# A ring of 19 weight tiles in place of 15, and the expert gather set between weight tiles

## The chip, the core and the metric

The kernel runs on one core of one Trainium2 chip. The metric is the device time of one execution in microseconds (us), lower is better. All inputs lie in the chip's memory (HBM) in the layout that the host prepared; the kernel is one launch.

## The reference, cut to what matters

The model is a decoder trunk of two layers on 256 tokens of width 1024. Each layer has a mixer and then a channel mixer. Layer 0 has a dense SwiGLU; layer 1 has a mixture of eight experts, each token sent to two of them. The change touches only that last part:

```python
def moe_swiglu(x, w_router, w1, w3, w2):
    t = x.reshape(bn * s, d)
    logits = (t @ w_router).astype(jnp.float32)
    top_val, top_idx = lax.top_k(logits, TOP_K)
    top_w = jax.nn.softmax(top_val, axis=-1)
    combine = jnp.sum(jax.nn.one_hot(top_idx, N_EXPERTS) * top_w[..., None], axis=1)
    for e in range(N_EXPERTS):
        out = out + combine[:, e:e + 1] * swiglu(t, w1[e], w3[e], w2[e])
```

with `swiglu(x, w1, w3, w2) = (silu(x @ w1) * (x @ w3)) @ w2`. w1 and w3 of an expert are 1024 x 3584, w2 is 3584 x 1024, all in float32: 44 MB an expert, 352 MB of the 476 MB that the kernel moves.

## The kernel before, in words

The first 466 us are the two mixers and the dense channel mixer; at their end stand the second mixer's output product (lines 147 to 150, out of the split activations hy_hi and hy_lo), the router and the top-2 choice. What follows works through the experts one after the other.

**Weight tiles.** An expert's weights come as 46 tiles: 32 of 128 x 1792 floats (917,504 bytes; for each half of the 3584 columns eight of w1 and then eight of w3) and 14 of 128 x 2048 floats (1 MB) of w2. That makes 368 loads for eight experts. The class Weights (line 938) issues them from SP's queue, in order, at line 953. FIRST (line 34) names the buffers in the order in which they are first filled; "x" is used once, and after that the other 15 names go round as a ring. A load may leave when the tile that was in its buffer has been used, and when the eighth load before it has landed. Buffers A0 to A4 are the ones that the first 466 us also load into; a0 to a3 and b0 to b5 lie in memory that the mixers used before (the pools mg, mc, mw, ra, rb are opened one after the other in the place of the mixers' pools, and ra, which holds a0 to a3, comes behind mg, mc and mw).

**An expert.** Tokens of an expert sit in slots, at most CAP = 96, as G = 3 groups of 32, or as two groups if 64 slots are enough: a register (mask, read out of cnt) picks one of two versions of the expert's code, one with G = 3 and one with G = 2. With these inputs experts 1, 3 and 5 take three groups and the others two. The first HEAD = 3 tiles of an expert are always done with three groups. g1 (line 1090) multiplies the expert's slots xg with a w1 or w3 tile: 4 G matmuls of 448 columns, each on 32 of TensorE's columns; a profile counts two records for each. silu and gate (lines 1108 and 1114) make ga out of the sums, turn (line 1118) transposes ga into gT through a misc bank, and g2 (line 1144) multiplies gT with the w2 tiles. yfin and scatter bring the result back to the tokens; the scatter's four pieces stand after the first three tiles of the next expert.

**The gather.** For a pair of experts make_p (line 1016) builds Pm, a one-hot matrix from tokens to 2 x 128 slots. gather(p, d2) (line 1068) makes one quarter of the pair's slots: for two of the eight blocks of the width, four matmuls each (high part and low part of the scaled tokens, for two halves of the tokens) of 128 rows by 256 columns into one misc bank, then two copies to XG, one on ACT and one on DVE, that take 96 of each 128 slots. The first pair's four quarters stand together ahead of the first expert's first tile (line 1283); the other pairs' quarters stand after tiles 1 to 4 of the second g1 of experts 1, 3 and 5, that is after the expert's tiles 10 to 13. htk_h and htk_l are the scaled tokens split into a rounded high part (ACT) and a low part (DVE, line 1028), out of four PSUM banks tk; DVE makes them in four pieces of 512 columns, with make_p between the second and the third.

**PSUM.** Eight banks: six acc (c0 to c5) are allocated first and two misc (m0, m1) last, so the misc banks are the ones that were used by the last two of the tk tiles.

**On the chip's names.** PE is TensorE, DVE VectorE, ACT ScalarE, POOL GpSimd; SP issues the weight loads.

Of the kernel before, what the change touches and what calls it, by code (L numbers as in the profile page):

```python
# [8 lines left out]
F32 = mybir.dt.float32  # L9
F32R = mybir.dt.float32r  # L10
# [18 lines left out]
CAP = 96  # L29
G = CAP // 32  # L30
FH = 1792
HEAD = 3
FQ = 448
FIRST = ("x", "b1", "b2", "a0", "a1", "A0", "a2", "A1", "a3", "A2", "b0", "A3", "A4", "b3", "b4", "b5")
AHEAD = len(FIRST) - 2
ADAS2 = (0, 0, 0)
ADAS3 = (1, 1, 3)
# [14 lines left out]
def tile_trunk(ctx: ExitStack, tc: tile.TileContext, xT_d, c_d, vecs_d, ada0_d, ada_d, adar_d, adah_d, s1_d, s2_d,  # L52
# [797 lines left out]
    def ffn_body(fk):  # L850
# [59 lines left out]
        for d in range(KB):  # L910
# [3 lines left out]
            if d % 2:  # L914
# [16 lines left out]
    rk_p = bank("o")  # L931

    slots = {k: (ra if k[0] == "a" else rb).tile([P, 2048], F32, name="raw", tag=k)
             for k in ("a0", "a1", "a2", "a3", "b0", "b1", "b2", "b3", "b4", "b5")}
    slots.update({f"A{i}": raw_a() for i in range(RAW1)})
    slots["x"] = const.tile([P, 2048], F32, name="raw", tag="ex")

# [23 lines left out]
    wts = Weights()  # L961
    wts.upto(len(FIRST))

    ga = {(h, g): mg.tile([P, FQ], F32, name="ga", tag=f"ga{h}{g}") for h in range(2) for g in range(G)}
    gT = [mg.tile([P, 14, CAP], F32, name="gT", tag=f"gT{h}") for h in range(2)]
    PTm = mg.tile([P, 2, T], F32R, name="PTm")
    XG = [mw.tile([P, 2, KB, CAP], F32, name="xg", tag=f"xg{p}") for p in range(2)]
    scr = XG[1].rearrange("p e k s -> p (e k s)")
    Pm = mw.tile([P, 2, 2, P], F32R, name="Pm")
    Qw = mw.tile([P, 2, 2, P], F32, name="Qw")  # L970
    wsl = mw.tile([P, 2], F32, name="ws")
# [22 lines left out]
    for t in range(2):  # L994
# [14 lines left out]
    nc.vector.scalar_tensor_tensor(rk, rk_p[:, 0:16].rearrange("p (t e) -> p t e", t=2), 1.0, sel,  # L1009
                                   op0=OP.add, op1=OP.mult)  # L1010

    def make_p(p):
        return nc.vector.tensor_tensor(Pm, iotas[:, None, None, :].to_broadcast([P, 2, 2, P]),
                                       rk[:, :, 2 * p:2 * p + 2, None].to_broadcast([P, 2, 2, P]),
                                       op=OP.is_equal)

    tw = mc.tile([P, 2, 2], F32, name="tw")
    cmx = mc.tile([P, 8], F32, name="cmx")
    htk_h = mc.tile([P, 2, D], F32R, name="htk_h")
    htk_l = mc.tile([P, 2, D], F32R, name="htk_l")  # L1020
    for j in range(2):
        if j:
            p_ins = make_p(0)
        for t in range(2):
            hi = htk_h[:, t, 512 * j:512 * j + 512]
            nc.scalar.activation(hi, tk[j][t], AF.Copy, scale=rt[:, t:t + 1])
            with tc.issue_after((p_ins if j else sel_ins).ins):
                nc.vector.scalar_tensor_tensor(htk_l[:, t, 512 * j:512 * j + 512], tk[j][t], rt[:, t:t + 1],
                                               hi.bitcast(F32), op0=OP.mult, op1=OP.subtract)
# [12 lines left out]
    nc.vector.tensor_scalar(many[:, 7:8], many[:, 7:8], -1.0, 384.0, op0=OP.mult, op1=OP.add)  # L1042
    nc.vector.tensor_scalar(cmx[:, 2:3], cmx[:, 0:1], CAP + 0.5, many[:, 7:8], op0=OP.is_gt, op1=OP.mult)
    nc.vector.tensor_add(cmx[:, 1:2], cmx[:, 1:2], cmx[:, 2:3])
    nc.vector.tensor_copy(cnt, cmx)
    nc.vector.tensor_sub(tw, mx[:, :, 0:2], mx[:, :, 0:1].to_broadcast([P, 2, 2]))
    fin = nc.scalar.activation(tw, tw, AF.Exp)
    tables(fin, SILU)
# [8 lines left out]
    pps.close()  # L1057
    pm = moe.enter_context(tc.tile_pool(name="pm", bufs=1, space=PSUM, reuse_waits="tile"))

    acc = [pm.tile([P, 512], F32, name="acc", tag=f"c{i}") for i in range(6)]  # L1060
    ms_ = [pm.tile([P, 512], F32, name="misc", tag=f"m{i}") for i in range(2)]
    turn_ = [0]

    def misc():
        turn_[0] ^= 1
        return ms_[turn_[0]]

    def gather(p, d2):
# [9 lines left out]
        tv = tp.rearrange("p (d e s) -> p d e s", d=2, e=2)  # L1078
        for dd in range(2):
            d = 2 * d2 + dd  # L1080
            sh = mods(1, 3)[:, d:d + 1]
            if dd:
                r = nc.vector.tensor_scalar(XG[p % 2][:, :, d], tv[:, dd, :, 0:CAP], sh, None, op0=OP.add)
            else:
                nc.scalar.activation(XG[p % 2][:, :, d], tv[:, dd, :, 0:CAP], AF.Identity, bias=sh)
        return r

    ahead = []

# [24 lines left out]
    def gate(h, banks, G):
        for g in range(G):
            nc.vector.tensor_mul(ga[h, g], banks[g][:, 0:FQ], ga[h, g])  # L1116

    def turn(h, g):
        tp = misc()
        for b in range(4):  # L1120
            o = 128 * b if b < 3 else FQ - P
            nc.tensor.transpose(tp[:, b * P:(b + 1) * P], ga[h, g][:, o:o + P], ident)  # L1122
        sl = slice(32 * g, 32 * g + 32)
        nc.scalar.copy(gT[h][:, 0:12, sl].rearrange("p (c b) s -> p b c s", c=4),  # L1124
                       tp[:, 0:384].rearrange("p (b c s) -> p b c s", b=3, c=4))
        tl = tp[:, 384:512].rearrange("p (u v s) -> p u v s", u=2, v=2)
        for v in range(2):
            nc.vector.tensor_copy(gT[h][64 * v:64 * v + 64, 12:14, sl], tl[64:128, :, v])  # L1128
# [179 lines left out]

    for e in range(NE):
        lo, hi = (acc[0:3], acc[3:6]) if e % 2 == 0 else (acc[3:6], acc[0:3])  # L1310
        heavy = (mask >> e) & 1
# [5 lines left out]
        fill = {0: (0,), 1: (1, 2), 2: (3,)} if e else {}  # L1317
        g1(e, lo, {k: lambda cs=cs: [scatter(c) for c in cs] for k, cs in fill.items()}, G, 0, HEAD)
# [110 lines left out]
```

## Time and profile before

| what | us |
|---|---|
| median of three runs | 1343.88 |
| the three runs | 1343.88, 1343.93, 1340.54 |
| the profiled execution, own time | 1339.97 |
| its span in the trace | 1338.3 |
| PE busy in the span | 1261.2 (94%) |
| DVE busy | 488.5 (37%) |
| ACT busy | 308.4 (23%) |
| bytes moved by DMA | 476.01 MB, 356 GB/s over the span |

The span is the time from the first to the last instruction that the profiler saw; the execution's own time is 1.7 us more. A busy PE counts the time in which matmuls stream, also where one slow clock makes them last longer, so 94% is not 94% of what TensorE could do. The page cuts the span into 40 slices of 33.5 us each; slice 0 begins at 0 us and slice 14 at 468 us, about where the first expert begins.

### The profile page before, as it was taken

To read this page: it belongs to the slowest core of one execution; us is meant where nothing else is said; L and a number is where in the kernel's file an instruction comes from. 1 tells how busy PE (TensorE), PEld (TensorE's weight loads), DVE (VectorE), ACT (ScalarE), POOL (GpSimd) and SP (SyncE) were. 2 spreads that over 40 slices of the span, in tenths; PEclk is the share of its full clock that TensorE was granted. 3 is DMA by queue.
4 is the path that set the end of the run, shared out by engine and by line. 5 is a ranking of instruction groups with operands and counts; after the bars stand their busy time and mean duration, and the time that the engine had idled before them with its cause. 6 is when DMAs were issued, how large, how long until landed. Compare 5 with 4: busy or idle time off the path is not lost. (4 is left out here: it accounts for less than half of the span.)

```text
span 1338.3 us, 26935 instructions
## 1 busy us (share of the span) xinstructions
PE 1261.2 (94%) x11847; PEld 713.7 (53%) x11847; DVE 488.5 (37%) x940; ACT 308.4 (23%) x521; POOL 14.4 (1%) x42
## 2 busy tenths in 40 slices
PE   7999999999999999899999989999989999998985
PEld 6888799999888943243333334333324333333322
DVE  7899888886678421011101111101101111111012
ACT  5764544444476310001000001000000100000101
POOL 3000000000000000000000000000000000000000
PEclk9999999999989989999999989999999999998998
DMA  9868799887454959999998999998999999899993
GB/s 368 341 222 299 270 371 353 333 307 255 161 216 158 407 195 426 424 423 425 423 372 360 426 422 424 426 411 323 425 425 422 426 424 367 350 426 423 425 427 146
DMA packets 72208, 476.01 MB, mean 356 GB/s; under 512 B 8097, under 2 KB 9265, under 8 KB 44802
## 3 DMA queue, kind: packets, MB, share of 16 engines
q1 hardware_dynamic: 71568, 473.07, 88.0%
q8 instruction: 104, 1.70, 0.5%
q0 software_dynamic: 352, 0.84, 0.2%
q14 instruction: 38, 0.31, 0.1%
q10 hardware_dynamic: 146, 0.09, 0.0%
HBM read 472.92 MB, written 1.05 MB: 354 GB/s over the span
## 5 line engine op out<-in xcount | busy, mean ns | idle before, releaser
L1096 PE MATMUL acc<-raw,xg 128*32 128x448 f32 x4984 | 497.4, 552 | 19.0 <-issue 16.4
L1096 PEld LDWEIGHTS acc<-raw,xg 128*32 128x32 f32 x4984 | 164.7, 112 | 321.1 <-issue 304.4
L1154 PE MATMUL acc<-raw,gT 128*32 128x512 f32 x2128 | 238.7, 594 | 13.0 <-DMA raw<-in_moe_dram 12.8
L118 DVE TENSOR_TENSOR wlo<-raw,whi 128x1024 fp32r<-128x1024 f32 (+2 forms) x138 | 159.4, 1163 | 49.7 <-ACT whi L116 47.7
L116 ACT CAST whi<-raw 128x1024 fp32r<-128x1024 f32 (+2 forms) x138 | 137.3, 999 | 119.6 <-PE bk_b L148 74.2
L1154 PEld LDWEIGHTS acc<-raw,gT 128*32 128x32 f32 x2128 | 65.1, 110 | 170.5 <-issue 143.3
L147 PE MATMUL bk_b<-hy_hi,whi 128*128 128x256 f32 (+1 forms) x528 | 128.0, 282 | 3.9 <-DVE Am L610 2.6
L148 PE MATMUL bk_b<-hy_lo,whi 128*128 128x256 f32 (+1 forms) x528 | 126.1, 280 | 0.0
L223 DVE SCALAR_TENSOR_TENSOR junk<-raw,exA 128x1024 bf16<-128x1024 f32 x88 | 107.9, 1226 | 1.4 <-DMA raw<-in_ada_dram 0.5
L147 PEld LDWEIGHTS bk_b<-hy_hi,whi 128*128 128x128 f32 (+1 forms) x528 | 96.9, 185 | 5.7 <-DVE Am L610 2.8
L148 PEld LDWEIGHTS bk_b<-hy_lo,whi 128*128 128x128 f32 (+1 forms) x528 | 96.9, 185 | 0.5 <-DVE hy_lo L397 0.2
L1124 ACT COPY gT<-misc 128x384 f32<-128x384 f32 x38 | 18.2, 480 | 318.1 <-PE misc L1122 297.4
L1116 DVE TENSOR_TENSOR ga<-acc,ga 128x448 f32<-128x448 f32 x38 | 23.7, 625 | 168.9 <-PE acc L1096 166.2
L1110 ACT ACTIVATE ga<-acc 128x448 f32<-128x448 f32 x38 | 20.7, 544 | 241.7 <-PE acc L1096 241.4
L1169 DVE SCALAR_TENSOR_TENSOR yhl<-acc,ws,yhl 128x512 fp32r<-128x512 f32 x11 | 8.3, 751 | 185.3 <-ACT yhl L1168 185.3
L150 PE MATMUL bk_b<-hy_hi,wlo 128*128 128x256 f32 (+1 forms) x528 | 74.4, 280 | 0.0
L147 PE MATMUL bk_o<-hy_hi,whi 128*128 128x256 f32 x256 | 65.7, 285 | 4.8 <-ACT hy_hi L396 4.8
L148 PE MATMUL bk_o<-hy_lo,whi 128*128 128x256 f32 x256 | 65.6, 283 | 0.6 <-DVE hy_lo L397 0.3
L150 PEld LDWEIGHTS bk_b<-hy_hi,wlo 128*128 128x128 f32 (+1 forms) x528 | 66.0, 185 | 0.0
L1128 DVE COPY gT<-misc 64x64 f32<-64x64 f32 x76 | 17.2, 227 | 120.9 <-ACT gT L1124 119.9
L1185 DVE SCALAR_TENSOR_TENSOR xT<-misc,modc,xT 128x256 f32<-128x256 f32 x60 | 26.7, 481 | 80.4 <-PE misc L1180 80.3
L150 PE MATMUL bk_o<-hy_hi,wlo 128*128 128x256 f32 x256 | 54.8, 285 | 0.0
(272 smaller groups left out, 1065.8 us busy)
## 6 DMA issues: line engine op xcount, KB each, us to landing
raw<-in_moe_dram SPq DMA_DIRECT2D x256, 896.0 KB, 14.6
raw<-in_moe_dram SPq DMA_DIRECT2D x112, 1024.0 KB, 17.7
raw<-in_ada_dram SPq DMA_DIRECT2D x44, 1024.0 KB, 7.2
raw<-in_ffn_dram SPq DMA_DIRECT2D x33, 1024.0 KB, 6.7
raw<-in_s_dram SPq DMA_DIRECT2D x16, 776.0 KB, 6.4
raw<-in_s_dram SPq DMA_DIRECT2D x12, 1024.0 KB, 4.9
raw<-in_wo_dram SPq DMA_DIRECT2D x8, 1024.0 KB, 4.8
raw<-in_adah_dram SPq DMA_DIRECT2D x2, 1024.0 KB, 6.2
```

The costliest lines, as they stand in the source:

```text
L116: self.hi_ins = nc.scalar.copy(hi[:, :n], raw[:, c0:c1])
L118: self.lo_ins = nc.vector.tensor_sub(lo[:, :n], raw[:, c0:c1], hi[:, :n].bitcast(F32))
L147: nc.tensor.matmul(out, lhsT=wh, rhs=xh, start=start, stop=False, skip_group_check=True)
L148: nc.tensor.matmul(out, lhsT=wh, rhs=xl, start=False, stop=False, skip_group_check=True)
L150: nc.tensor.matmul(out, lhsT=wl, rhs=xh, start=False, stop=stop, skip_group_check=True)
L223: nc.vector.scalar_tensor_tensor(junk, row, 1.0, cond, op0=OP.mult, op1=OP.mult, accum_out=dots[:, l, 8 * g + k:8 * g + k + 1])
L1096: mm = nc.tensor.matmul(banks[g][32 * c:32 * c + 32, 0:FQ], lhsT=xg[:, k, 32 * g:32 * g + 32], rhs=raw[:, FQ * c:FQ * c + FQ], start=(k == ...
L1110: sil = nc.scalar.activation(ga[h, g], banks[g][:, 0:FQ], AF.Silu)
L1116: nc.vector.tensor_mul(ga[h, g], banks[g][:, 0:FQ], ga[h, g])
L1124: nc.scalar.copy(gT[h][:, 0:12, sl].rearrange("p (c b) s -> p b c s", c=4), tp[:, 0:384].rearrange("p (b c s) -> p b c s", b=3, c=4))
L1154: nc.tensor.matmul(yy[n][32 * c:32 * c + 32, :], lhsT=gt[:, blk, 32 * g:32 * g + 32], rhs=rhs, start=(j == 0 and (n == 1 or bb == 0)), sto ...
L1185: nc.vector.scalar_tensor_tensor(xT[:, d], tps[h][:, cols], mods(1, 5)[:, d:d + 1], xT[:, d], op0=OP.mult, op1=OP.add)
```

## The change

The diff below is cut to its core. What it does, part by part:

- FIRST gets 20 names: "x", used once, and 19 that go round. b6 to b9 are new, and the order of the names changes; a1 is the fifth name, a0 the last.
- ga has one set of three tiles instead of one for each half; XG is one tile with three slots, an expert's slot being e % 3, instead of two tiles with two; make_p makes two compares where the pair's slots come in the other order (pair).
- The second argument of the launch, dynamic_dma_scratch_size=2048, makes GpSimd's descriptor ring smaller.
- The eight PSUM banks are allocated in another order: m0 second, m1 sixth.
- A gather's matmul takes 2 x 96 columns of Pm instead of 2 x 128.
- The first pair's quarters are put between tiles: quarter 0 ahead of the first expert's first tile, quarters 1, 2 and 3 after its first, second and third tile. The load of mask follows the first tile, and weights() the third.
- The low parts are made in eight pieces of 256 columns (rest), with rk and make_p after the first of them and the counting between the fourth and the fifth.

```diff
-FIRST = ("x", "b1", "b2", "a0", "a1", "A0", "a2", "A1", "a3", "A2", "b0", "A3", "A4", "b3", "b4", "b5")
+FIRST = ("x", "b9", "b2", "b3", "a1", "a2", "A0", "a3", "A1", "b0", "A2", "b1", "A3", "A4", "b4", "b5", "b6", "b7", "b8",
+         "a0")
...
-             for k in ("a0", "a1", "a2", "a3", "b0", "b1", "b2", "b3", "b4", "b5")}
+             for k in [f"a{i}" for i in range(4)] + [f"b{i}" for i in range(10)]}
...
-    ga = {(h, g): mg.tile([P, FQ], F32, name="ga", tag=f"ga{h}{g}") for h in range(2) for g in range(G)}
+    ga = {g: mg.tile([P, FQ], F32, name="ga", tag=f"ga{g}") for g in range(G)}
...
-    XG = [mw.tile([P, 2, KB, CAP], F32, name="xg", tag=f"xg{p}") for p in range(2)]
-    scr = XG[1].rearrange("p e k s -> p (e k s)")
+    XG = mw.tile([P, 3, KB, CAP], F32, name="xg")
+    scr = XG[:, 2].rearrange("p k s -> p (k s)")
...
+    def rest(t, q, after):
+        cs, half = slice(T * q, T * q + T), slice(T * (q % 2), T * (q % 2) + T)
+        with tc.issue_after(after.ins):
+            return nc.vector.scalar_tensor_tensor(htk_l[:, t, cs], tk[q // 2][t][:, half], rt[:, t:t + 1],
+                                                  htk_h[:, t, cs].bitcast(F32), op0=OP.mult, op1=OP.subtract)
...
+    r_ins = rest(0, 0, sel_ins)
+    with tc.issue_after(r_ins.ins):
+        r_ins = nc.vector.scalar_tensor_tensor(rk, rk_p[:, 0:16].rearrange("p (t e) -> p t e", t=2), 1.0, sel,
+                                               op0=OP.add, op1=OP.mult)
...
+    def pair(p):
+        return sorted((2 * p, 2 * p + 1), key=lambda e: e % 3)
...
+    with tc.issue_after(r_ins.ins):
+        r_ins = make_p(0)
+    for t, q in ((1, 0), (0, 1), (1, 1)):
+        r_ins = rest(t, q, r_ins)
+    with tc.issue_after(r_ins.ins):
+        nc.vector.max(cmx, rk_p[:, 16:24])
...
-    nc.vector.tensor_copy(cnt, cmx)
+    c_ins = nc.vector.tensor_copy(cnt, cmx)
+    for t, q in ((0, 2), (1, 2), (0, 3), (1, 3)):
+        c_ins = rest(t, q, c_ins)
...
-    acc = [pm.tile([P, 512], F32, name="acc", tag=f"c{i}") for i in range(6)]
-    ms_ = [pm.tile([P, 512], F32, name="misc", tag=f"m{i}") for i in range(2)]
+    banks = [pm.tile([P, 512], F32, name="acc" if n[0] == "c" else "misc", tag=n)
+             for n in ("c0", "m0", "c1", "c2", "c3", "m1", "c4", "c5")]
+    acc, ms_ = [banks[i] for i in (0, 2, 3, 4, 6, 7)], [banks[i] for i in (1, 5)]
...
     def gather(p, d2):
-        tp = misc()
+        a, b = (e % 3 for e in pair(p))
+        tp = misc().rearrange("p (d t) -> p d t", d=2)[:, :, 0:2 * CAP]
...
-                    nc.tensor.matmul(tp[:, dd * T:(dd + 1) * T], lhsT=src[:, t, d * P:(d + 1) * P], rhs=Pm[:, t],
+                    nc.tensor.matmul(tp[:, dd], lhsT=src[:, t, d * P:(d + 1) * P], rhs=Pm[:, t, :, 0:CAP],
...
-    for d2 in range(4):
-        last = gather(0, d2)
-        if d2 == 0:
-            mask = nc.values_load(cnt[0:1, 1:2], min_val=0, max_val=256 + 127,
-    with tc.issue_after(last.ins):
-        weights()
...
+        if e == 0:
+            gather(0, 0)
+            g1(0, lo, {0: lambda: gather(0, 1)}, G, 0, 1)
+            mask = nc.values_load(cnt[0:1, 1:2], min_val=0, max_val=256 + 127,
...
+            fill = {k: lambda k=k: gather(0, k + 1) for k in (1, 2)}
+        g1(e, lo, fill, G, k0, HEAD)
         if e == 0:
+            weights()
...
-    nc = _bacc.Bacc("TRN2", target_bir_lowering=False, num_devices=1)
+    nc = _bacc.Bacc("TRN2", target_bir_lowering=False, num_devices=1, dynamic_dma_scratch_size=2048)
```

## Rows read from the trace of the kernel before

**Rows 1.** The profile's page: its span, and what DMA moved in 40 equal slices.
```profile
span 1338.3 us, 26935 instructions
...
GB/s 368 341 222 299 270 371 353 333 307 255 161 216 158 407 195 426 424 423 425 423 372 360 426 422 424 426 411 323 425 425 422 426 424 367 350 426 423 425 427 146
```

**Rows 2.** The chain that ended last: start us, us, what it was.
```profile
1241.69 18.00 DMA raw<-in_moe_dram
...
1296.45 19.46 DMA raw<-in_moe_dram
...
1316.05 1.98 PE acc L1154 x16
```

**Rows 3.** Busy times by stretch (us): length, engines' busy time, TensorE clock, DMA share, GB/s.
```profile
469.20:483.50 14.30, 11.89 (x86) 7.85 (x90) 6.47 (x22) 2.89 (x5) 0.00 (x0) 0.75 0.01 2
483.50:505.00 21.50, 21.50 (x232) 7.41 (x228) 0.40 (x1) 1.09 (x2) 0.00 (x0) 1.00 0.93 365
505.00:560.00 55.00, 52.46 (x502) 16.60 (x494) 5.96 (x16) 3.00 (x6) 0.00 (x0) 1.00 1.01 425
640.00:705.00 65.00, 63.76 (x608) 22.52 (x604) 9.64 (x22) 2.81 (x5) 0.00 (x0) 1.00 0.97 386
705.00:715.00 10.00, 10.00 (x112) 3.51 (x108) 0.55 (x2) 1.09 (x2) 0.00 (x0) 1.00 0.78 273
1080.00:1141.00 61.00, 59.77 (x556) 20.90 (x552) 8.99 (x21) 2.81 (x5) 0.00 (x0) 0.98 0.96 378
1141.00:1152.00 11.00, 11.00 (x116) 3.46 (x112) 0.00 (x0) 1.09 (x2) 0.00 (x0) 0.96 0.79 281
1152.00:1316.00 164.00, 148.05 (x1384) 48.43 (x1376) 16.96 (x41) 9.07 (x16) 0.00 (x0) 0.98 1.00 419
```

**Rows 4.** SP's queue, waits at 600 to 712, then 1215 to 1300: us, times, longest.
```profile
SPq L953 <- PE acc L1096: 61.8, 29, 6.5
...
SPq L953 <- DMA raw<-in_moe_dram: 53.7, 29, 2.6
```

**Rows 5.** PE's waits at 538 to 562, 764 to 779 and 982 to 997.
```profile
PE acc L1154 <- DMA raw<-in_moe_dram: 2.5, 5, 0.6
...
PE acc L1154 <- DMA raw<-in_moe_dram: 0.6, 1, 0.6
...
PE acc L1154 <- DMA raw<-in_moe_dram: 1.6, 3, 0.6
```

**Rows 6.** PE's timeline, last tiles of expert 0: start, us, what, records, idle before.
```profile
537.84 10.51 PE L1154 MATMUL acc<-raw,gT 128*32 128x512 f32 x96
548.73 1.92 PE L1154 MATMUL acc<-raw,gT 128*32 128x512 f32 x16 [0.38 <-DMA raw<-in_moe_dram]
```

**Rows 7.** PE's timeline in expert 3, with gather quarters between tiles.
```profile
804.66 7.70 PE L1096 MATMUL acc<-raw,xg 128*32 128x448 f32 x80
...
813.41 2.46 PE L1096 MATMUL acc<-raw,xg 128*32 128x448 f32 x24
...
816.94 2.46 PE L1096 MATMUL acc<-raw,xg 128*32 128x448 f32 x24
```

**Rows 8.** TensorE's weight loads (PEld) in the second mixer.
```profile
455.01 0.19 PEld L147 LDWEIGHTS bk_o<-hy_hi,whi 128*128 128x128 f32 x1
455.13 0.19 PEld L148 LDWEIGHTS bk_o<-hy_lo,whi 128*128 128x128 f32 x1
...
456.20 0.98 PEld L789 LDWEIGHTS bk_b<-rtA,xT 128*128 128x128 f32 x8
```

**Rows 9.** The timeline of all engines around the first gather.
```profile
459.25 0.20 POOL L973 MEMSET xg<- 128x128 bf16 x1 [118.85 <-PE bk_o L150]
...
469.46 0.68 DVE L1013 TENSOR_TENSOR Pm<-iotas,rk 128x512 fp32r<-128x512 f32 x1
470.06 1.41 DVE L1028 SCALAR_TENSOR_TENSOR htk_l<-bk_o,rt,htk_h 128x512 fp32r<-128x512 f32 x2
...
471.61 0.77 PE L1075 MATMUL misc<-Pm,htk_h 128*128 128x256 f32 x2 [3.14 <-DVE cmx L1031]
```

More of the change, by code (lines that the diff above doesn't have):

```diff
@@ L1008, in tile_trunk @@
     rk = mc.tile([P, 2, NE], F32, name="rk")
-    nc.vector.scalar_tensor_tensor(rk, rk_p[:, 0:16].rearrange("p (t e) -> p t e", t=2), 1.0, sel,
-                                   op0=OP.add, op1=OP.mult)
-    def make_p(p):
-        return nc.vector.tensor_tensor(Pm, iotas[:, None, None, :].to_broadcast([P, 2, 2, P]),
-                                       rk[:, :, 2 * p:2 * p + 2, None].to_broadcast([P, 2, 2, P]),
-                                       op=OP.is_equal)
+    htk_h = mc.tile([P, 2, D], F32R, name="htk_h")
@@ new lines, in tile_trunk @@
+    htk_l = mc.tile([P, 2, D], F32R, name="htk_l")
+    def rest(t, q, after):
[3 more added lines that the diff above has]
+                                                  htk_h[:, t, cs].bitcast(F32), op0=OP.mult, op1=OP.subtract)
+    for j in range(2):
+        for t in range(2):
+            nc.scalar.activation(htk_h[:, t, 512 * j:512 * j + 512], tk[j][t], AF.Copy, scale=rt[:, t:t + 1])
@@ new lines, in tile_trunk @@
+    r_ins = rest(0, 0, sel_ins)
[4 more added lines that the diff above has]
+        return sorted((2 * p, 2 * p + 1), key=lambda e: e % 3)
+    def make_p(p):
+        a, b = pair(p)
+        for es in ((a, b),) if a < b else ((a,), (b,)):
+            q, n = es[0] != a, len(es)
+            r = nc.vector.tensor_tensor(Pm[:, :, q:q + n], iotas[:, None, None, :].to_broadcast([P, 2, n, P]),
+                                        rk[:, :, es[0]:es[0] + n, None].to_broadcast([P, 2, n, P]), op=OP.is_equal)
+        return r
@@ L1017, in tile_trunk @@
     tw = mc.tile([P, 2, 2], F32, name="tw")
     cmx = mc.tile([P, 8], F32, name="cmx")
[L1019 to L1029, printed above, removed]
@@ L1031, in tile_trunk @@
-    nc.vector.max(cmx, rk_p[:, 16:24])
+    with tc.issue_after(r_ins.ins):
[4 more added lines that the diff above has]
+        nc.vector.max(cmx, rk_p[:, 16:24])
     many = mc.tile([P, NE], F32, name="many")
@@ L1074, in gather @@
                 for t in range(2):
-                    nc.tensor.matmul(tp[:, dd * T:(dd + 1) * T], lhsT=src[:, t, d * P:(d + 1) * P], rhs=Pm[:, t],
+                    nc.tensor.matmul(tp[:, dd], lhsT=src[:, t, d * P:(d + 1) * P], rhs=Pm[:, t, :, 0:CAP],
                                      start=(n == 0), stop=(n == 3), skip_group_check=True)
                     n += 1
-        tv = tp.rearrange("p (d e s) -> p d e s", d=2, e=2)
+        tv = tp.rearrange("p d (e s) -> p d e s", e=2)
         for dd in range(2):
@@ L1082, in gather @@
             if dd:
-                r = nc.vector.tensor_scalar(XG[p % 2][:, :, d], tv[:, dd, :, 0:CAP], sh, None, op0=OP.add)
+                r = nc.vector.tensor_scalar(XG[:, a:b + 1:b - a, d], tv[:, dd], sh, None, op0=OP.add)
             else:
-                nc.scalar.activation(XG[p % 2][:, :, d], tv[:, dd, :, 0:CAP], AF.Identity, bias=sh)
+                nc.scalar.activation(XG[:, a:b + 1:b - a, d], tv[:, dd], AF.Identity, bias=sh)
         return r
@@ L1090, in g1 @@
     def g1(e, banks, fill, G, k0=0, k1=KB):
-        xg = XG[e // 2 % 2][:, e % 2]
+        xg = XG[:, e % 3]
         for k in range(k0, k1):
@@ L1109, in silu @@
         for g in range(G):
-            sil = nc.scalar.activation(ga[h, g], banks[g][:, 0:FQ], AF.Silu)
+            sil = nc.scalar.activation(ga[g], banks[g][:, 0:FQ], AF.Silu)
         if e == NE - 1 and h == 1:
@@ L1115, in gate @@
         for g in range(G):
-            nc.vector.tensor_mul(ga[h, g], banks[g][:, 0:FQ], ga[h, g])
+            nc.vector.tensor_mul(ga[g], banks[g][:, 0:FQ], ga[g])
     def turn(h, g):
@@ L1121, in turn @@
             o = 128 * b if b < 3 else FQ - P
-            nc.tensor.transpose(tp[:, b * P:(b + 1) * P], ga[h, g][:, o:o + P], ident)
+            nc.tensor.transpose(tp[:, b * P:(b + 1) * P], ga[g][:, o:o + P], ident)
         sl = slice(32 * g, 32 * g + 32)
@@ L1281, in finish @@
                 nc.sync.dma_start(out=out_d[:, k], in_=o[:, k])
-    for d2 in range(4):
-        last = gather(0, d2)
-        if d2 == 0:
-            mask = nc.values_load(cnt[0:1, 1:2], min_val=0, max_val=256 + 127,
-                                  skip_runtime_bounds_check_because="a bit for each expert")
-    with tc.issue_after(last.ins):
-        weights()
     def expert(e, lo, hi, G):
@@ L1310, in tile_trunk @@
         lo, hi = (acc[0:3], acc[3:6]) if e % 2 == 0 else (acc[3:6], acc[0:3])
+        k0 = 0 if e else 1
+        if e == 0:
+            gather(0, 0)
+            g1(0, lo, {0: lambda: gather(0, 1)}, G, 0, 1)
+            mask = nc.values_load(cnt[0:1, 1:2], min_val=0, max_val=256 + 127,
+                                  skip_runtime_bounds_check_because="a bit for each expert")
         heavy = (mask >> e) & 1
@@ L1316, in tile_trunk @@
         ahead.append(hint)
-        fill = {0: (0,), 1: (1, 2), 2: (3,)} if e else {}
-        g1(e, lo, {k: lambda cs=cs: [scatter(c) for c in cs] for k, cs in fill.items()}, G, 0, HEAD)
+        if e:
+            fill = {k: lambda cs=cs: [scatter(c) for c in cs] for k, cs in enumerate(((0,), (1, 2), (3,)))}
+        else:
+            fill = {k: lambda k=k: gather(0, k + 1) for k in (1, 2)}
+        g1(e, lo, fill, G, k0, HEAD)
         if e == 0:
+            weights()
             yhl = const.tile([P, 2, 2, 512], F32R, name="yhl", tag="ex")
```

## The prediction

> **What bounds the kernel now.** I read the page's slices first: from slice 15 on the transfers run at 422 to 427 GB/s, except in slice 14 and in three dips, slices 20 and 21, 27, 33 and 34 [rows 1]. These slices are the experts. The chain that ended last is a string of weight transfers to 1315.9 us, then 22 us of scatter, norm and stores that the change leaves alone [rows 2]. So the transfer queue sets the end, and the question is which of its gaps can close.
>
> The busy times by stretch show them [rows 3]. 469.2 to 483.5: the ring is full and nothing moves. 505 to 560: 425 GB/s, and PE is idle for 2.5 us. 640 to 705 and 705 to 715: 386 and 273 GB/s, while PE is busy for all but 1.2 us. 1080 to 1141 and 1141 to 1152 repeat this, and slice 27 is its like [rows 1]. Against 425 GB/s such a dip loses 65 x (1 - 386/425) + 10 x (1 - 273/425) = 6.0 + 3.6 = 9.6 us. The queue's waits tell why: between 600 and 712 it waits for PE to give a slot back, at the end for the landing of the eighth transfer before [rows 4].
>
> The two sides take turns. Experts 1, 3 and 5 need three groups of tokens (24 matmul records a tile, 7.70 x 24/80 = 2.3 us [rows 7], against 2.16 us for 917,504 bytes at 425 GB/s), and their gathers and scatters come on top: PE falls behind until it holds the whole ring, and the queue stops. The other five need two groups, 16 records, and PE catches up; in their last tiles it waits for each transfer [rows 5].
>
> **The ring, 15 slots to 19.** At a dip, transfer n leaves when PE frees tile n-15; after the change, when it frees tile n-19. So at the same moment of PE the queue is four transfers further: 4 x 2.16 = 8.6 us. After the last dip (expert 6, 1152 us) the stretch to 1316 runs at 419 GB/s and is the queue's alone, so these 8.6 us reach the end.
>
> They add up over the dips only as far as PE can follow, since between two dips PE is the path. It gains what it now waits for at the ends of experts 2 and 4: 0.6 us in one wait and 1.6 us in three [rows 5]. A wait costs more than its idle time, as a tile's records last 1.92 us and an unhindered step takes (10.51 - 1.92)/5 = 1.72 us [rows 6]: 0.2 us more each. That makes 0.8 and 2.2 us. The waits in expert 7 are the queue's stretch and count in the 8.6. Sum so far: 8.6 + 0.8 + 2.2 = 11.6 us. This is less than half of the three dips together, since closing a dip makes PE the bound.
>
> **The first expert.** Its waits are worth 2.5 + 5 x 0.2 = 3.5 us [rows 5]. I expect hardly any of it. The pools ahead of a0 shrink by three ga tiles and one XG slot, 3 x 1,792 + 3,072 = 8,448 bytes. By the program's allocation a0 began until now exactly where hy_lo ends; a1, 8,192 bytes above a0, will begin 256 bytes below that end. Memory of an old tile is given out when all uses of that tile are over: the memset of line 973, which writes into hy_hi, came at 459.25, released by the last product of the mixer [rows 9]. a1 is the fifth load in FIRST and the queue is in order, so all that stand behind it wait. Transfers then run from about 461 us (an estimate: the release and 2 us until data flows) without a pause: to 505 us 44 x 425 GB/s = 18.7 MB, 20 tiles, and four before makes 24. Today it is 16 tiles and 21.5 x 365 GB/s = 7.8 MB, 8.5 tiles [rows 3], 24.5 in all. So the tail of expert 0 gets its tiles when it gets them today, and I take 0 to 1 us.
>
> **The start of PE.** The gather waits until 471.61 for the last low part, which frees its bank; Pm is ready at 470.14 [rows 9]. With banks 5 and 1, free by then, with half-size pieces and with Pm after the first of them, the first quarter can start about 2 us earlier. The first tile follows one quarter instead of four, but the other quarters stand between the next tiles, so what PE has done by the third tile is the same. It gains 1 to 3 us (an estimate, the clock's half-speed stretch up to 476 us included), all of which the tail of expert 0 takes back as a wait for transfers. Cover gone, it would be worth up to 3 us.
>
> **The gather's matmuls.** Their moving side goes from 256 to 192 columns: 8 in a quarter, four quarters in experts 1, 3 and 5, 96 on PE's path. A quarter costs 3.53 - 2.3 = 1.2 us now [rows 7]. No row has a rounded matmul under 256 columns. From below: a load of a fresh 128 x 128 block, with only 8 columns behind it, recurs every (0.98 - 0.19)/7 = 0.113 us; the 256-column ones follow each other by 0.12 us [rows 8], and 192/256 of it is 0.09. From above: unrounded f32 moves 448 columns in 7.70/20 x 2 = 0.77 us [rows 7], for 192 columns 0.33 us. I take 0.12, no change: each of these matmuls brings a fresh block, and the row nearest to it is the one that shows the floor. The ends are -2.9 us (96 x 0.03) and +20 us (96 x 0.21).
>
> The Trainium skill, page "TensorE: Matmul & The Clock Gate", section "Back-to-back issue gap", gives N/2.4 + 2.5 ns from one matmul to the next on a warm array, 82.5 ns for 192 columns. By it the change would give 96 x 0.0375 = 3.6 us more than my sum. Its section on LDWEIGHTS has the load take P/1.2 ns, 107 ns for 128 columns whatever moves behind it, and the floor of 0.113 us in this trace sides with that one.
>
> **No cost.** One set of ga for both halves: the transposes that read it end in the third tile of the next product, and the next SiLU comes after its eighth. Two compares instead of one for pairs whose slots wrap, strided evictions, smaller low parts: DVE is busy for 6 of 55 us [rows 3]. The mask is loaded after the first tile, behind PE's queued work. The smaller descriptor ring of GpSimd serves six small loads far from any path.
>
> **Sum.** 8.6 + 0.8 + 2.2 + 0.5 = 12.1 us, less or more by the DMA's own jitter. The profiled execution took 1339.97 us, which gives 1327.9. The median of the three runs stands 3.9 us above it, and I predict against the median: 1343.9 - 12.4, rounded to 1331 us; own range 1326 to 1336.
>
> **Rivals.**
> 1. *The loads aren't held at a1.* Then 20 tiles are in by 478 us (469.2 + 4 x 2.16), the next slot comes back at about 481, expert 0 loses its 3.5 us of waits and PE keeps 1 to 2 of its earlier start: gain 17 us, 1327. For it: nothing in the trace settles how much of hy_lo must be free. Against it: line 973's release. Chance 0.15.
> 2. *Narrow matmuls are cheaper* (192/256 of the time): gain 15 to 16 us, 1328. Against it: the 0.113 us floor. Chance 0.10.
> 3. *Narrow matmuls are slow: slower than before.* If a rounded matmul under 256 columns streams like unrounded f32, 0.33 us, the three gathers cost 96 x 0.21 = 20 us on PE's path, and the first gather 32 x 0.21 = 6.7 us, of which expert 0's slack takes about 5. Net 12 - 20 - 2 = -10 us: 1354, in experts 1, 3 and 5 alone, quarters of 2.9 us instead of 1.2. It decides from 0.24 us a matmul on (96 x 0.12 = 11.6). For it: every rounded matmul in this trace has 256 or 512 columns, so none speaks against it. Against it: the floor is one of loading, and nothing shows a step in the streaming. Chance 0.22.
> 4. *It doesn't do what it says*: the freed time is spent again, by a price of about 0.22 to 0.26 us or by PE waiting elsewhere: 1340 to 1347. Chance 0.10.
>
> **How the numbers follow.** My forecast gets the remaining 0.43. A measurement of this kernel can tell about 0.3%, 4 us, from no change (its three runs span 3.4 us). Faster: 0.43 + 0.15 + 0.10 = 0.68; within 0.3%: 0.10; slower: 0.22. The range 1323 to 1351 holds the faster cases and the even one, and reaches towards rival 3 without holding it: about 0.2 is left out.
>
> **What would show it.** Right: the dips after experts 1, 3 and 5 shrink from about 9.6 us to 1 to 3; PE has no waits for transfers in the tails of experts 2 and 4; transfers stand still at 440 to 459 us instead of 469 to 483, and the queue names the wait at the fifth load; quarters in experts 1, 3 and 5 still cost about 1.2 us. Wrong: quarters of 2 us or more (rival 3); a queue that still stops for 9 us behind heavy experts (the ring did not bind); transfers through 459 us (rival 1); or PE waiting in experts 2 and 4 as before.

## The result and the profile after

The changed kernel took 1329.75 us (median of 4 runs, 1324.85 to 1331.87) against 1343.91 before: 0.989 of the time, 95% interval 0.986 to 0.993, 14.2 us less by the medians. The prediction was 1331; that the two lie 1.3 us apart is more than four runs that span 7.0 us can tell. The profiled execution of the changed kernel is its slowest run, 1331.87 us with a span of 1330.2.

Of its page, the span and the transfers in 40 slices:

```profile
span 1330.2 us, 26955 instructions
...
GB/s 370 344 190 301 278 362 356 323 315 276 155 218 212 92 424 425 426 423 425 425 424 392 426 423 424 425 425 339 423 424 422 426 424 412 344 427 422 424 427 124
```

The halt of the queue now stands in slice 13 (92 GB/s) and not in slice 14. The dip of slices 20 and 21 [rows 1] is nearly gone (slice 21: 392), those of slices 27 and 33, 34 are still there. Busy times by stretch of the changed kernel, columns as in [rows 3]:

```profile
443.00:461.00 18.00, 18.00 (x156) 18.00 (x155) 7.43 (x12) 5.69 (x10) 0.00 (x0) 1.00 0.00 1
461.00:505.00 44.00, 40.44 (x373) 20.69 (x375) 11.89 (x47) 7.66 (x15) 1.59 (x15) 0.88 0.98 407
505.00:560.00 55.00, 51.15 (x484) 15.84 (x480) 5.45 (x15) 3.00 (x6) 0.00 (x0) 1.00 1.01 425
640.00:705.00 65.00, 63.96 (x609) 22.28 (x601) 8.26 (x18) 2.81 (x5) 0.00 (x0) 0.99 1.01 425
705.00:715.00 10.00, 10.00 (x77) 4.11 (x80) 2.10 (x5) 0.00 (x0) 0.00 (x0) 0.71 0.88 345
860.00:923.00 63.00, 61.76 (x585) 21.94 (x585) 9.64 (x22) 2.81 (x5) 0.00 (x0) 1.00 1.00 410
923.00:932.00 9.00, 9.00 (x88) 3.01 (x84) 0.54 (x2) 0.75 (x2) 0.00 (x0) 0.84 0.60 204
1080.00:1141.00 61.00, 59.76 (x552) 20.75 (x548) 8.88 (x21) 2.81 (x5) 0.00 (x0) 0.97 0.95 391
1141.00:1152.00 11.00, 11.00 (x124) 3.58 (x120) 0.00 (x0) 1.09 (x2) 0.00 (x0) 1.00 0.91 327
```

And the two stretches around the dip behind expert 3 in the kernel before:

```profile
860.00:923.00 63.00, 61.77 (x576) 21.55 (x572) 8.96 (x21) 2.81 (x5) 0.00 (x0) 0.98 0.95 384
923.00:932.00 9.00, 9.00 (x100) 2.88 (x96) 0.00 (x0) 1.09 (x2) 0.00 (x0) 0.98 0.81 285
```

Against 425 GB/s the three dips lost 9.6, 6.1 + 3.0 = 9.1 and 6.7 + 3.7 = 10.5 us before [rows 3], 29.2 in all. They now lose 1.9, then 2.2 + 4.7 = 6.9, then 4.9 + 2.5 = 7.4 us, 16.2 in all: 13.0 us are closed. At the start a little is given back: almost nothing moves from 443 to 461, and then 44 x 407 GB/s = 17.9 MB come until 505, 19.5 tiles, with the four before 23.5 against 24.5. One tile is 2.2 us.

The queue's waits, from 455 to 520 us and from 600 to 712 us (us, times, longest):

```profile
SPq L954 <- PE bk_o L151: 19.0, 1, 19.0
...
SPq L954 <- DMA raw<-in_moe_dram: 54.2, 30, 3.3
SPq L954 <- PE acc L1172: 20.1, 13, 2.2
SPq L954 <- PE acc L1114: 15.5, 10, 9.0
```

One wait of 19.0 us for the second mixer's last products is the halt. The view names line 151, the last of them; the timeline shows the load going before line 151's records ended and right behind the last of line 149, which reads hy_lo and ended at 461.14:

```profile
460.86 0.28 PE L149 MATMUL bk_o<-hy_lo,whi 128*128 128x256 f32 x1
...
460.97 0.40 PE L151 MATMUL bk_o<-hy_hi,wlo 128*128 128x256 f32 x2
...
461.17 38.47 SPq L954 DMA_DIRECT2D raw<-in_moe_dram  x24
```

Its first packet moved at 462.13, 1.0 us later. Around the first dip the queue now waits mostly for its own transfers, 54 us, where it waited for PE only [rows 4].

The two executions have a different start: the router's first step on ACT comes at

```profile
466.06 0.26 ACT L838 ACTIVATE rt<-bk_b,eps_c 128x2 f32<-128x2 f32 x1 [4.60 <-PE bk_b L789]
```

before, and 1.85 us later in the changed kernel, a lag that is there within the first 60 us, in parts that the change leaves alone; over all 14 profiled executions this step comes at 464.4 to 470.9 us. The changed kernel's timeline from there, and the last tile's matmuls in its chain of waits:

```profile
467.91 0.26 ACT L839 ACTIVATE rt<-bk_b,eps_c 128x2 f32<-128x2 f32 x1 [4.35 <-PE bk_b L790]
...
470.78 0.69 DVE L1034 TENSOR_TENSOR Pm<-iotas,rk 128x512 fp32r<-128x512 f32 x1
...
471.62 0.71 PE L1093 MATMUL misc<-Pm,htk_h 128*128 128x192 f32 x2 [1.16 <-DVE Pm L1034]
...
474.12 1.65 DVE L1016 SCALAR_TENSOR_TENSOR htk_l<-bk_o,rt,htk_h 128x256 fp32r<-128x256 f32 x4
```

```profile
1306.74 1.98 PE acc L1172 x16
```

From that step on ACT to the end of the last tile's matmuls it is 1318.03 - 466.06 = 851.97 us before [rows 2] and 1308.72 - 467.91 = 840.81 after: 11.2 us less. That is the number to hold against the prediction's sum; 1.85 us of later start and a tail that took 21.5 us in place of 20.3 make the spans differ by only 8.1.

### The profile page after: what moved, and what is told of

Same layout as the page of the kernel before. It is cut to its first block, busy times and chain, and to the rows that moved or that the text cites. A ratio compares the mean times of both kernels' runs of the same rounds, so it can differ in the third digit from the quotient of the medians.

```text
span 1330.2 us, 26955 instructions
## 1 busy us (share of the span) xinstructions
PE 1262.4 (95%) x11847; PEld 719.4 (54%) x11847; DVE 488.3 (37%) x945; ACT 308.2 (23%) x521; POOL 14.3 (1%) x42
## 4 chain that ended last, share of the span: by engine, by line
PE 85%; DMA 6%; DVE 5%; issue 2%; ACT 2%; ACTq 0%; DVEq 0%; SPq 0%
PE acc L1114 35%; PE acc L1172 15%; DMA raw<-in_moe_dram 6%; PE bk_b L148 4%; PE bk_b L151 4%; PE bk_b L149 4%; PE bk_o L148 3%; PE bk_o L149 3%; PE bk_o L151 3%; PE misc L1198 2%; PE misc L1140 2%; PE misc L1093 1%; PE bk_b L379 1%; PE bk_b L155 1%; PE bk_b L156 1%
## 5 line engine op out<-in xcount | busy, mean ns | idle before, releaser
L1114 PE MATMUL acc<-raw,xg 128*32 128x448 f32 x4984 | 498.1, 555 | 14.4 <-issue 14.3
```

## The experiments

All ratios are to the kernel before, run beside each kernel on the same chip; its medians there were 1344.73 (beside the first four kernels), 1342.28 (the next four) and 1343.22 (the last four).

| kernel | median us (range) | ratio, 95% interval |
|---|---|---|
| e1, ring of 15 | 1343.32 (1339.09 to 1348.47) | 0.9987 (0.9969 to 1.0004) |
| e2, ring alone | 1328.01 (1324.78 to 1331.12) | 0.9865 (0.9838 to 0.9892) |
| e3, 256 columns | 1328.98 (1326.22 to 1331.32) | 0.9874 (0.9848 to 0.9900) |
| e4, a1 late | 1322.53 (1316.36 to 1325.32) | 0.9824 (0.9795 to 0.9852) |
| e5, ring of 17 | 1331.28 (1327.52 to 1334.32) | 0.9915 (0.9894 to 0.9935) |
| e6, ring alone, a1 late | 1322.84 (1319.37 to 1324.37) | 0.9847 (0.9827 to 0.9868) |
| e7, ring of 15, a1 late | 1340.09 (1335.99 to 1344.73) | 0.9984 (0.9969 to 0.9998) |
| e8, no low part | 1330.77 (1327.96 to 1334.22) | 0.9916 (0.9896 to 0.9937) |
| f1, the changed kernel again | 1328.94 (1320.32 to 1333.44) | 0.9879 (0.9848 to 0.9910) |
| f2, short low part | 1326.17 (1321.91 to 1331.29) | 0.9868 (0.9844 to 0.9893) |
| f3, a1 late again | 1323.31 (1320.29 to 1323.99) | 0.9837 (0.9816 to 0.9859) |
| f4, ring alone, a1 late, again | 1325.87 (1316.27 to 1327.36) | 0.9849 (0.9821 to 0.9877) |

**Is it the ring?** First the changed kernel with only the ring undone:

```diff
-FIRST = ("x", "b9", "b2", "b3", "a1", "a2", "A0", "a3", "A1", "b0", "A2", "b1", "A3", "A4", "b4", "b5", "b6", "b7", "b8", "a0")
+FIRST = ("x", "b9", "b2", "b3", "a1", "a2", "A0", "a3", "A1", "b0", "A2", "b1", "A3", "A4", "b4", "a0")
```

> The changed kernel with b5 to b8 taken out of FIRST, so 15 buffers go round instead of 19; everything else stays changed. If the ring carries the gain (my theory): a transfer again leaves when PE frees the tile 15 before, 4 x 2.16 = 8.6 us later at the same moment of PE, and PE waits at the ends of experts 2 and 4 come back (2 to 3 us): 1340 to 1342 us. If the gather's new place, its 192 columns and the earlier first tile carry it (rival): 1329 to 1332 us.

It is no faster than the kernel before by more than can be told; its median is 1.3 us above the expected range. In its trace the queue waits for PE alone again around the first dip, and PE waits for transfers again at the end of expert 2 (the queue from 600 to 715 us, then PE from 750 to 785):

```profile
SPq L954 <- PE acc L1114: 64.7, 29, 9.0
SPq L954 <- PE acc L1172: 32.5, 14, 2.9
...
PE acc L1172 <- DMA raw<-in_moe_dram: 1.6, 3, 0.6
```

Then the reverse, the ring put into the kernel before, with the memory that makes room for it and nothing of the gather's parts:

```diff
-FIRST = ("x", "b1", "b2", "a0", "a1", "A0", "a2", "A1", "a3", "A2", "b0", "A3", "A4", "b3", "b4", "b5")
+FIRST = ("x", "b9", "b2", "b3", "a1", "a2", "A0", "a3", "A1", "b0", "A2", "b1", "A3", "A4", "b4", "b5", "b6", "b7", "b8", "a0")
...
-    ga = {(h, g): mg.tile([P, FQ], F32, name="ga", tag=f"ga{h}{g}") for h in range(2) for g in range(G)}
+    ga = {g: mg.tile([P, FQ], F32, name="ga", tag=f"ga{g}") for g in range(G)}
...
-    XG = [mw.tile([P, 2, KB, CAP], F32, name="xg", tag=f"xg{p}") for p in range(2)]
+    XG = mw.tile([P, 3, KB, CAP], F32, name="xg")
...
+    nc = _bacc.Bacc("TRN2", target_bir_lowering=False, num_devices=1, dynamic_dma_scratch_size=2048)
```

> The kernel before with the new FIRST and the memory that it needs (one set of ga, XG with three slots, the smaller descriptor ring), but with the old gather: four quarters ahead of the first tile, 256 columns, low parts in four pieces, old order of banks. My theory: 1330 to 1332 us, as the first tile starts some 2.5 us later, which expert 0's waits for transfers take up, and twelve gather quarters cost 0.07 us more each. Rival (the gather's parts are needed for the gain): 1335 us or more.

The ring alone gives the whole gain, and comes out 2 us below its expected range. What the gather's parts add to a held queue can't be seen in these runs.

**What is a slot worth?**

```diff
-FIRST = ("x", "b9", "b2", "b3", "a1", "a2", "A0", "a3", "A1", "b0", "A2", "b1", "A3", "A4", "b4", "b5", "b6", "b7", "b8", "a0")
+FIRST = ("x", "b9", "b2", "b3", "a1", "a2", "A0", "a3", "A1", "b0", "A2", "b1", "A3", "A4", "b4", "b5", "b6", "a0")
```

> The changed kernel with b7 and b8 taken out of FIRST: 17 buffers go round. If a slot is worth a transfer at the dip (theory), two slots less cost 2 x 2.16 = 4.3 us, and PE's waits at the ends of experts 2 and 4 come back in part (0 to 2 us): 1333 to 1337 us, about midway between 15 slots (1343.3) and 19 (1329.8). If the gain comes from a threshold that 17 already passes: 1329 to 1331 us; if it needs all 19: 1341 us or more.

By the ratio, 0.9915 x 1343.9 = 1332.5 us, 17 slots lie nearer to 19 than midway, and both this and the median are a little below the expected range. The queue's waits of this kernel from 600 to 712 us:

```profile
SPq L954 <- PE acc L1114: 53.7, 25, 9.0
SPq L954 <- PE acc L1172: 32.5, 14, 2.9
SPq L954 <- DMA raw<-in_moe_dram: 8.3, 5, 1.8
```

It waits for PE for 54 us in the w1 and w3 tiles, against 64.7 with 15 slots and 15.5 with 19. The traces also show the lead itself: how long a tile has been there when PE begins it. For the 32nd tile of expert 4, which PE begins 500.4 us behind the router's step both with 17 and with 19 slots, the transfer had landed at 488.4 with 17 and at 483.5 with 19, so the leads are 12.0 and 16.9 us. With 15 slots the lead is 7.8 (e1; 8.2 in the kernel before and 7.2 in e7, described below). The last two slots are worth 4.9 us and the first two 4.2, 9.1 for four or 2.3 a slot, against 2.16 forecast; kernels with 19 slots differ by 0.8 us among themselves (16.1 to 16.9), so there is no threshold between 15 and 19 to be seen, and no difference between the two pairs. By the ratios the first two give more at the end (9.7 us against 3.2, with 4 to 5 us of doubt on each). One reason is that PE's waits at the ends of experts 2 and 4, 1.6 and 1.0 us with 15 slots, are gone with 17, where the expectation had them come back in part; that this is the whole reason is not shown.

**Does the gather's width matter?**

```diff
-        tp = misc().rearrange("p (d t) -> p d t", d=2)[:, :, 0:2 * CAP]
+        tp = misc().rearrange("p (d t) -> p d t", d=2)
...
-                    nc.tensor.matmul(tp[:, dd], lhsT=src[:, t, d * P:(d + 1) * P], rhs=Pm[:, t, :, 0:CAP],
+                    nc.tensor.matmul(tp[:, dd], lhsT=src[:, t, d * P:(d + 1) * P], rhs=Pm[:, t],
...
```

> The changed kernel with the gather's matmuls at 256 columns again. A quarter should cost 3.53 - 2.3 us again against 3.46 - 2.3 with 192 columns in the changed kernel: 12 x 0.07 = 0.8 us on PE's path, so 1330 to 1331 us. If narrow matmuls were cheaper in proportion (rival 2 of the prediction) it would be 3 us or more: 1333 us.

Not at the end of the time: 1328.98 us, 1 us below the expected range. PE's timeline in expert 3, first the changed kernel's (192 columns), then this one's (256):

```profile
815.77 2.46 PE L1114 MATMUL acc<-raw,xg 128*32 128x448 f32 x24
818.16 0.47 PE L1093 MATMUL misc<-Pm,htk_h 128*128 128x192 f32 x2
818.46 0.39 PE L1093 MATMUL misc<-Pm,htk_l 128*128 128x192 f32 x2
818.69 0.39 PE L1093 MATMUL misc<-Pm,htk_h 128*128 128x192 f32 x2
...
819.23 2.46 PE L1114 MATMUL acc<-raw,xg 128*32 128x448 f32 x24
```

```profile
814.62 2.46 PE L1114 MATMUL acc<-raw,xg 128*32 128x448 f32 x24
...
818.15 2.46 PE L1114 MATMUL acc<-raw,xg 128*32 128x448 f32 x24
```

From one tile to the next, a quarter between them, it is 819.23 - 815.77 = 3.46 us with 192 columns and 818.15 - 814.62 = 3.53 with 256. Two matmuls of 192 columns follow each other's pair by 818.69 - 818.46 = 0.23 us, 0.115 each; with 256 it was 0.12 [rows 8]. Twelve quarters make 0.8 us, less than the runs can tell.

**What does the halt at a1 cost?**

```diff
-FIRST = ("x", "b9", "b2", "b3", "a1", "a2", "A0", "a3", "A1", "b0", "A2", "b1", "A3", "A4", "b4", "b5", "b6", "b7", "b8", "a0")
+FIRST = ("x", "b9", "b2", "b3", "a2", "A0", "a3", "A1", "b0", "A2", "b1", "A3", "A4", "b4", "b5", "b6", "b7", "b8", "a1", "a0")
```

> The changed kernel with a1 moved from fifth to second last in FIRST, so that nothing stands behind it while hy_lo is in use. My theory: transfers run on from 443 us instead of standing still to 461, 20 tiles are in by about 478 us, PE's waits in the last tiles of expert 0 go (3.9 us in 7 waits, with 0.2 us more each: 5 us), and as PE sets when the later dips end, the gain reaches the end: 1324 to 1326 us. Rival (the hold at a1 costs nothing, since the lead is lost again at the first dip and PE doesn't gain): 1329 to 1331 us.

> The changed kernel with a1 second last in FIRST, as before, now beside the changed kernel on one chip: 5 to 8 us under it, 1321 to 1325 us.

1322.5 us, 1.5 us below its expected range, and 1323.3 us, which is 5.6 us under the changed kernel on the same chip (f1). Two stretches of the first:

```profile
443.00:461.00 18.00, 18.00 (x154) 18.00 (x152) 6.91 (x9) 6.43 (x10) 0.00 (x0) 1.00 1.01 424
505.00:560.00 55.00, 55.00 (x540) 18.22 (x532) 6.37 (x16) 3.01 (x6) 0.00 (x0) 1.00 1.01 425
```

The transfers run through at 424 GB/s where nothing moved, and from 505 to 560 PE doesn't wait at all; in the changed kernel it did, in the last tiles of expert 0 (PE's waits from 538 to 562 us):

```profile
PE acc L1172 <- DMA raw<-in_moe_dram: 3.9, 7, 0.6
```

Counted from the router's step, the last tile of expert 7 ended 8.1 and 8.7 us earlier than in the changed kernel (832.65 in e4 and 831.39 in f3, against 840.75 and, in f1, 840.09). But both executions of this kernel came to that step late, at 470.4 and 470.9 us, and the lag was there before the edit can act: their first expert load left at 423.75 and 424.86 us, against 421.68. Whether the late start belongs to this kernel stays open. The dip behind expert 1 is back in it, 3.5 + 3.7 = 7.2 us (9.2 in f3) against 1.9 in the changed kernel. In e4:

```profile
640.00:705.00 65.00, 63.78 (x600) 22.49 (x596) 10.20 (x23) 2.82 (x5) 0.00 (x0) 0.98 0.98 402
705.00:715.00 10.00, 10.00 (x108) 3.33 (x104) 0.00 (x0) 1.09 (x2) 0.00 (x0) 0.94 0.78 266
```

With 15 slots going round the same edit does little, since the buffers run out anyway: the 17th load leaves at 478.53 us, when PE has given a slot back.

```diff
-FIRST = ("x", "b9", "b2", "b3", "a1", "a2", "A0", "a3", "A1", "b0", "A2", "b1", "A3", "A4", "b4", "b5", "b6", "b7", "b8", "a0")
+FIRST = ("x", "b9", "b2", "b3", "a2", "A0", "a3", "A1", "b0", "A2", "b1", "A3", "A4", "b4", "a1", "a0")
```

> The changed kernel with 15 buffers going round (without b5 to b8) and a1 second last: nothing is held, only the gather's parts and the order of FIRST differ from the kernel before. The first slot comes back about 3.3 us earlier than in the kernel before (end of the second tile at 14.0 against 17.4 us after the router), so transfers begin again 3 us earlier and expert 0 ends earlier by that: 1339 to 1342 us. Rival (the gather's parts are worth nothing, and the hold at a1 cost nothing with 15 slots): 1343 to 1345 us.

The median lies in the first theory's range. But it is 2.2 us under the kernel before on its chip, the interval reaches from 4.2 us to almost none (0.9998), and it overlaps that of e1; so the gain is small and hardly shown.

**The first tile's earlier start, with its cover gone.** The edit of e4 in the kernel of e2, run twice:

> The ring alone in the kernel before, with a1 moved to second last in FIRST; gather ahead of the first tile as before, at 256 columns. With a1 late there is no wait for transfers in expert 0 that would take up PE's later start, so by the prediction (cover gone, up to 3 us) this should cost 2 to 3.5 us against the changed kernel with a1 late (1322.5): 1324.5 to 1326 us. If the start of PE is worth nothing even then (rival): 1321 to 1323.5 us.

> The ring alone with a1 late and the old gather, as before, now beside the changed kernel with a1 late on one chip. If the earlier first tile is worth something once expert 0 has no wait for transfers: 2 to 3.5 us over it (the traces show 2.6 us at the third tile at the same clock). If it is worth nothing: the same.

The first run's median, 1322.84, fell into the rival's range: equal to e4's, which ran on another chip, though the ratios lie 3 us apart. Beside the changed kernel with a1 late on the same chip it is 1325.87 against 1323.31, 2.6 us slower, as the theory has it. The intervals overlap, so the size is likely and not settled. Not all of it is the start: the 256 columns of the old gather stand in these 2.6 us too, with about 0.8. At the end of expert 0, ahead of those quarters, the two traces part by 2.6 us (91.16 in f4 and 88.56 in f3 behind the router's step), those of e6 and e4 by 1.0.

**Is PE the bound in what is left of the dips?**

```diff
-            for src in (htk_h, htk_l):
+            for src in (htk_h,) if p else (htk_h, htk_l):
...
```

> The changed kernel without the low part in the gathers of experts 2 to 7: 4 instead of 8 matmuls a quarter. It leaves out part of the computation (the low part of the tokens of these experts) to shorten PE's path by 12 x 4 x 0.111 = 5.3 us and nothing else. If PE is what the queue waits for in the dips that are left (theory): 4 to 6 us less, 1324 to 1326 us. If the queue alone is the bound now (rival): 1328.5 to 1330.5 us.

No gain, as the rival had it. But the trace shows PE ahead: by the last tile of expert 4 it was 3.8 us further than in the changed kernel (523.80 against 527.55 us behind the router's step). Then, at the start of expert 5 (PE's timeline):

```profile
992.74 1.70 PE L1114 MATMUL acc<-raw,xg 128*32 128x448 f32 x2 [3.20 <-issue]
998.23 8.75 PE L1114 MATMUL acc<-raw,xg 128*32 128x448 f32 x70 [3.79 <-issue]
```

PE stops for 3.2 us as the changed kernel does, does two records, and stops again for 3.8 us, for nothing that the profile shows; a further stop of 1.5 us stands in expert 3. The page's group of these matmuls (last: idle before, by issue), first of the changed kernel, then of e8:

```profile
L1114 PE MATMUL acc<-raw,xg 128*32 128x448 f32 x4984 | 498.1, 555 | 14.4 <-issue 14.3
```

```profile
L1114 PE MATMUL acc<-raw,xg 128*32 128x448 f32 x4984 | 502.1, 555 | 19.3 <-issue 19.2
```

The idle time by issue grew from 14.3 to 19.2 us, about what the matmuls left out had saved. The stops that all kernels have stand between two experts, where the program leaves one version of an expert's code for the next; e8's program has fewer instructions. That the length brought the further stops is a guess. So the work was taken out again with every instruction kept:

```diff
+                    m, c = (32, 32) if p and src is htk_l else (P, 2 * CAP)
+                    rhs = Pm[:, t, 0, 0:32] if c == 32 else Pm[:, t, :, 0:CAP]
-                    nc.tensor.matmul(tp[:, dd], lhsT=src[:, t, d * P:(d + 1) * P], rhs=Pm[:, t, :, 0:CAP],
+                    nc.tensor.matmul(tp[0:m, dd, 0:c], lhsT=src[:, t, d * P:d * P + m], rhs=rhs,
```

> The changed kernel with the low part in the gathers of experts 2 to 7 cut to 32 rows and 32 columns. It leaves out nearly all of that low part but keeps every instruction, so the program's length and the places where its code is fetched stay as they are; in the run without the low part an extra stop for code at the start of expert 5 took 4 us. A short matmul should take about 0.03 to 0.06 us instead of 0.111: 12 x 4 x (0.05 to 0.08) = 2.4 to 3.8 us less of PE. If PE is what the queue waits for in the dips (theory): 2 to 4 us under the changed kernel of this call. If the queue alone is the bound (rival): no difference to it.

> The changed kernel again, as the baseline of the next three on the same chip: 1328 to 1331 us.

f2's page and its timeline in expert 3:

```profile
L1116 PE MATMUL acc<-raw,xg 128*32 128x448 f32 x4984 | 499.9, 556 | 14.1 <-issue 14.0
```

```profile
812.26 2.46 PE L1116 MATMUL acc<-raw,xg 128*32 128x448 f32 x24
...
815.44 2.46 PE L1116 MATMUL acc<-raw,xg 128*32 128x448 f32 x24
```

The idle time by issue is back at 14.0, a quarter's step is 3.18 us instead of 3.46 (12 x 0.28 = 3.4 us), and the median is 2.8 us under that of f1. The theory expected this, the rival no difference; the intervals (0.984 to 0.989 and 0.985 to 0.991) overlap, so the end of the time leans to the theory and doesn't settle it. The profiled pair leans less: 1.5 us of its difference lies ahead of the router's step, and from that step the last tile of expert 7 ended only 0.4 us earlier (839.66 against 840.09), with other draws of the clock on the way. That e8 meets its second stop in each execution was not shown: one was profiled.

## Why the prediction was right, and where it was not

**The ring, 8.6 us: right.** The runs with 15 and with 19 slots, each way round, leave the ring as the cause. When PE begins expert 4's 32nd tile, the tile had been there for 8.2 us before and for 16.9 after: 8.7 us for four slots.

**PE's waits at the ends of experts 2 and 4, 3.0 us: right.** From an expert's 32nd tile to the end of its last, PE needs 27.17 us where it waits for nothing, which is what the changed kernel takes in both. Before it was 28.33 and 29.65: 3.6 us are gone, and they come back with 15 slots (e1: 29.56 and 28.54).

**The sum, 12.1 us: right, with some luck.** PE ended expert 5 at 1125.45 - 467.91 = 657.54 us after the router's step, 3.1 us earlier than before (1126.74 - 466.06 = 660.68), and the queue was four transfers further beyond that: 3.1 + 8.6 = 11.7 us, measured 11.2. These 3.1 us are near the forecast partly by chance. Expert 0 gave 0.7 and the waits 3.6; a stretch of low clock in expert 2 took 2.9 back, and shorter ways into experts 3 and 5 (0.9 and 0.8), which nobody forecast, made up for more than half of it. The forecast itself takes 12.4 from the median where its sum is 12.1, and gives no reason for the 0.3.

**Expert 0, 0 to 1 us: right, and for the reason given.** The queue stood at the fifth load until 461.17, the wait was for the product that reads hy_lo (the 2 us that the prediction then gives until data flows are 1.0 in the trace), and PE waited in the last tiles for 3.9 us in 7 waits (2.5 in 5 before). Expert 0 ended 0.7 us earlier after the router's step. Rival 1 priced loads that aren't held at 4.6 us above the forecast (17 against 12.4); f3 against f1 measures 5.6.

**PE's start: right in size.** The first quarter came 3.71 us after the router's step (471.62 - 467.91) instead of 5.55, and the fourth tile ended 2.5 us earlier (18.6 against 21.1 us behind that step). Expert 0's waits took it back; with them gone the old gather costs about 2.6 us (f4 against f3), some 0.8 of it by its columns, so the start is worth about 2, within the 3 us that the prediction gave; the overlap of the intervals leaves the size open.

**The gather's matmuls, no change: right.** 0.115 us at 192 columns; a quarter is 0.07 us shorter. Rivals 2 and 3 fall. The Trainium skill, page "TensorE: Matmul & The Clock Gate", would have 82.5 ns by the formula in its section "Back-to-back issue gap" and 107 ns by that in "LDWEIGHTS (loading the stationary operand)"; the 115 ns of this trace side with the second. The first section itself says that its formula leaves out the weight load and counts too little at small widths, which the prediction didn't say.

**The dips: the step that failed.** The prediction looked for dips of 1 to 3 us behind experts 1, 3 and 5. That is so behind expert 1 (1.9 us), and there by luck; the others kept 6.9 and 7.4. It contradicted its own sum: four slots put the queue four transfers further once. Past the first dip the lead is there already, so a later dip shrinks only by what PE gains between the two. The sum, made from lead and PE, had this right, the list of signs had not. Behind expert 1 the dip was small because the halt at a1 had kept the queue behind: in e4 and f3, with the same 19 slots and no halt, it is 7.2 and 9.2 us again, in a kernel that is faster.

**What a profiled pair hides.** In the execution profiled, TensorE's clock was low at the start of expert 2, where it was not in the kernel before (704 to 712 us, before and then after; the third number from the end is the granted clock):

```profile
704.00:712.00 8.00, 8.00 (x88) 2.93 (x90) 1.54 (x4) 0.55 (x1) 0.00 (x0) 1.00 0.61 193
```

```profile
704.00:712.00 8.00, 8.00 (x51) 3.99 (x53) 2.58 (x6) 0.00 (x0) 0.00 (x0) 0.58 0.85 338
```

51 records in place of 88 in 8 us, at a mean granted clock of 0.58, a stretch in which the clock was at its lower level (1.2 GHz) and then at the full one. It followed the scatter between two experts, where PE waits for DVE in short turns (0.57 and 0.47 us); in the kernel before the same waits (0.58, 0.47 and 0.19 us) were followed by no fall. The scatter and the two tiles after it took 2.9 us more than before (11.3 against 8.4). Of the 14 profiled executions eleven have this stretch and three (the kernel before, e2 and e7) don't, with the gather in either place on both sides; what decides it stays open. So a single pair of traces can differ by some 3 us in one place, and not every such difference belongs to the change.

**A version faster than both.** The changed kernel with a1 second last in FIRST: 1322.5 and 1323.3 us, 0.982 and 0.984 of the time before, with the halt gone.

## What to carry to other kernels

When two engines take turns at being late, count a deeper ring as a lead that is earned once, at the last place where the ring fills before the end, plus what the other engine stops waiting for; the earlier dips don't add up, and those that remain are no sign that the ring failed. Here a slot was worth 2.2 to 2.3 us of lead, about one transfer. When buffers of a later stage overlay those of an earlier one, put the buffers that come free last at the end of an in-order queue's first round: here 256 bytes of overlap in the fifth of 20 held everything behind it for 18 us and 5.6 us of the end. Before judging by the end time what less work on an engine is worth, look whether its idle time grew by the same amount.

## What the runs showed that was not expected

From the end of one expert to the end of the third tile of the next, the executions differ far more than elsewhere: into experts 1, 3, 5 and 7 this took 10.6 to 15.5 us over the 14 profiled executions, and 17.4 once (e8, expert 5), of which three tiles of 24 records need 6.9 (3 x 2.3). The parts are the stop by issue, 3 to 4.3 us (5.7 and 5.6 at two places of e1), and a stretch of low clock behind it. Over the four places together it is 46.9 to 59.0 us: a spread of 12 us, while runs of one kernel differ by 7 us (the changed kernel) to 13 us (f1), and more than any single part of this change. What sets the length of a stop is not shown.
